# First MLP's second product in seven block products for three of four hidden chunks, and half rows of modulation weights in slots of their own

## The chip, the cores and the metric

One core of a Trainium2 chip runs the whole forward pass of two layers. The metric is the time of one execution on the device in microseconds (us), the median of several runs. The engines named here are TensorE (PE, with its weight loads shown as PEld), VectorE (DVE), ScalarE (ACT), GpSimd (POOL) and SyncE (SP). SP and POOL each have a queue from which transfers are issued.

## The reference, cut to what matters

512 tokens of width 1024 pass through two layers. Layer 0 mixes Fourier channels with neighbourhood attention, layer 1 mixes by pooling, and each layer ends with the same kind of MLP. All numbers are fp32.

```python
def sq_relu_mlp(u, w1, w2):          # u: 512 x 1024, w1: 1024 x 4096, w2: 4096 x 1024
    a = jnp.maximum(u @ w1, 0.0)
    return (a * a) @ w2

for l in range(DEPTH):               # DEPTH = 2
    mod = sc @ w_mod[l] + b_mod[l]   # w_mod[l]: 1024 x 6144
    sh1, sc1, g1, sh2, sc2, g2 = split(mod, 6)
    ...
    h = h + g1 * y                   # y: the mixer's output
    h = h + g2 * sq_relu_mlp(modulate(rms_norm(h, norm2_g[l]), sh2, sc2), w_mlp1[l], w_mlp2[l])
```

A modulation vector `mod` of 1024 numbers is called (l, v) below, v from 0 to 5; (0, 5) is the gate g2 of layer 0.

## The kernel before, in words

Every large product is made of fp32r numbers in two parts: a value is split into a rounded high part (a copy on ACT) and the rest (a subtraction on DVE), and a product is three matmuls, high by high, high by low and low by high (`mm3`, L99 to 103; in the seven-product code the three stand at L1670 to L1672). A matmul has 128 x 128 stationary and 128 x 512 moving numbers where nothing else is said.

The order on each engine is written out by hand. `later` puts a small job on a list with a due time, `tick` (L82) runs at most one due job and then `W.beat()`; both count in `pe[0]`, the matmul time issued so far. `flush` runs all jobs that are left. So jobs and weight splits fall between the matmuls in the order in which the program emits them, and each engine keeps that order.

`Feed` (the object `W`, L113) brings in weights. There are five raw slots of 512 KB (`wr`). `load` issues transfers on SP in the order of `W.items` as long as a slot is free. `one("w")` splits the oldest piece into `wh` (ACT, L204) and `wl` (DVE, L207), and there is room for eight split pieces in the MLPs. `one("m")` takes a row of `w_mod` (128 x 1024, 512 KB): `mac` (L272) multiplies it by the conditioning value and adds it to `macc` on DVE (L278, L280). After eight rows `finish` sums over the partitions with matmuls against ones (L291) and `columns` turns the result with two transposes (L312). `beat` takes a piece when it was issued more than `lead` ago, and a row when the last one is more than `gap` ago. All pieces and rows use the same five raw slots.

The MLP of layer 0 (`mlp`, L1400) goes through four chunks of 1024 hidden units. For each chunk the first product makes eight tiles of 128 hidden units x 512 tokens from 192 matmuls; `act` (L1391) squares them and splits them into `ah` and `al` (DVE L1396, L1397). The second product makes eight tiles of 128 output columns, 192 matmuls again, and `add_h` (L918) adds each one, times the gate, to the token stream `hT`, which is kept transposed (channels on partitions). The last chunk's second product is done in two halves of 256 tokens, so that the next mixer's norm can start.

The MLP of layer 1 (`mlp_blocks`, L1616) writes the second product of each chunk in another way. Its left side, 512 tokens x 1024 hidden units, and its right side are each cut in two by two blocks, and the product is made of seven products of blocks (the Winograd form of Strassen's scheme) in the order "11", "T3", "T1", "T2", "22", "T4", "21", 24 matmuls each. Sums of left blocks are made on DVE in `E` (L1639) and split (`parts`, L96 and L97). Sums of right blocks, that is of weights, are made while they are brought in: a second transfer issued from POOL adds to a raw slot (`add`, L144). The pieces T1, T2 and T4 stand in the same slot one after another: T2's transfer adds to T1's data once that is split, T4's to T2's. The seven results are summed in five accumulators `ac` (L1688 to L1692), with tokens on partitions; at the end the output is stored straight from there, with the token stream turned by `turn` (transposes L1705).

The rows of `w_mod` for the vectors (1, v) are items between the MLP's weights of layer 0.

Of the kernel before, what the change touches and what calls it, by code (L numbers as in the profile page):

```python
# [17 lines left out]
P = 128  # L18
# [20 lines left out]
def body(ctx: ExitStack, tc: tile.TileContext, x, c, cx, c_ctx, w_mod, b_mod, norm1_g, norm2_g,  # L39
# [38 lines left out]

    def later(fn, after=0.0):
# [33 lines left out]
    class Feed:  # L113
# [3 lines left out]
        def __init__(self, nr):  # L117
# [8 lines left out]

            self.place, self.chain = {}, {}
# [19 lines left out]
        def m(self, l, v):  # L147
            for k in range(KT):
                src = w_mod[l, P * k:P * (k + 1), D * v:D * (v + 1)].unsqueeze(1)
                yield ["m", (l, v, k), src, (P, 1, D), None, 0.0]  # L150

        def load(self, n=None):
            while self.loaded < len(self.items) and (n is None or n > 0):
# [29 lines left out]
                if n is not None:  # L183
                    n -= 1

        def one(self, kind, auto=True, eng=None):
# [48 lines left out]
        def beat(self):  # L235

            self.lows()
            for kind in ("w", "m"):
                if not (self.hold and kind == "w") and self.wait[kind] and pe[0] - self.wait[kind][0][5] > self.lead:
# [4 lines left out]
                    elif pe[0] - self.last > (min(self.gap, 2.0) if self.wait["m"][0][1][0:2] == (0, 5) and self.gap < 100 else self.gap):  # L244
# [27 lines left out]
        def mac(self, key, w):  # L272
            l, v, k = key
# [7 lines left out]
            if k == KT - 1:  # L281
                self.fin = (l, v)
                later(lambda: self.fin == (l, v) and self.finish(), {(0, 5): 9.0}.get((l, v), 6.0 if l else 3.5))

        def finish(self):
# [9 lines left out]
            later(lambda: self.columns(l, v, ms), 7.0 if l or v == 5 else 1.5)  # L295
# [13 lines left out]
        def columns(self, l, v, ms):  # L309
            pt = bank("t", "pmvt")  # L310
            for b in range(2):
# [4 lines left out]
                                    bcol(l, v).rearrange("p (g b) -> p g b", g=4), op=ALU.add)  # L316
            if v == 4:
# [876 lines left out]
    W.behind, W.lead = True, 8.0  # L1194
# [7 lines left out]
    Y = Slots(tail, "mz", {"v": 4, "y": 6, "z": 4, "bd": 1})  # L1202
# [105 lines left out]

    def w1_items(l):
        w1v = w1[l].rearrange("(k p) n -> p k n", p=P)  # L1310
        w2v = w2[l].rearrange("(c k p) n -> c p k n", p=P, k=KT)
        for c4 in range(4):
            for q in range(4):
                for e in range(2):
                    c0 = half_columns(c4, q) if l else c4 * 1024 + q * 256
                    yield ("w1", l, c4, q, e), w1v[:, 4 * e:4 * e + 4, c0:c0 + 256], 4, 256, None
            if l:
# [6 lines left out]
    def half_columns(c4, q):  # L1324

        return 2048 * (q % 2) + 512 * c4 + 256 * (q // 2)
# [33 lines left out]
    bd = Y("bd", "bd", shape=(P, 4 * BAND_W))  # L1360
    nc.sync.dma_start(bd, kband)
# [29 lines left out]
    def act(ps, slot):  # L1391
        a, a2 = M("x", "a"), M("x", "a2")
        th, tl = slot("ah"), slot("al")
        nc.scalar.activation(a, ps, AF.Relu)  # L1394
        nc.scalar.activation(th, a, AF.Square)
        nc.vector.tensor_tensor(a2, a, a, op=ALU.mult)  # L1396
        nc.vector.tensor_tensor(tl, a2, th.bitcast(F32), op=ALU.subtract)  # L1397
        return th, tl

    def mlp(l, v, slot, nB, tile_done, half_done, between=None):  # L1400

        vh, vl = v
        waiting = []

        def w1_mm(ps, c4, q, m, c0, c1, ks=range(KT)):
            for k in ks:
                hi, lo = W.get(("w1", l, c4, q, k // 4))
                mm3(ps[:, c0:c1], hi[:, k % 4, m * P:(m + 1) * P], lo[:, k % 4, m * P:(m + 1) * P],
                    vh[k][:, c0:c1], vl[k][:, c0:c1], k == 0, k == KT - 1)
                if k % 2 and k < 6 and c1 == N:  # L1410
                    tick()

        def w2_mm(ps, c4, q, m, ah, c0, c1):
            for k in range(KT):
                hi, lo = W.get(("w2", l, c4, q, k // 4))
                mm3(ps[:, 0:c1 - c0], hi[:, k % 4, m * P:(m + 1) * P], lo[:, k % 4, m * P:(m + 1) * P],
                    ah[k][0][:, c0:c1], ah[k][1][:, c0:c1], k == 0, k == KT - 1)
                if k % 2 and k < 6:
                    tick()

        def free(name, c4, q):
            for e in range(2):
                W.done((name, l, c4, q, e))

        for c4 in range(4):
            ah = []
            first = 0
# [484 lines left out]
```

## Time and profile before

| | |
|---|---|
| median of 3 runs | 1024.47 us (1024.01 to 1027.89) |
| the profiled execution | 1022.89 us, span 1021.0 us |
| PE busy | 993.0 us (97%) |
| DVE busy | 663.2 us (65%) |
| ACT busy | 453.4 us (44%) |
| POOL busy | 121.1 us (12%) |
| moved by DMA | 164.94 MB, 162 GB/s over the span |
| granted TensorE clock | 0.994 |

The layer-0 MLP runs from 287 us to 650 us of the span, the layer-1 MLP from 676 us to the end. Busy times of matmuls overlap, since they are pipelined; the distance from one matmul's start to the next is the better measure. The share of DMA is the mean over 16 DMA engines.

### The profile page before, as it was taken

The page shows a single profiled execution, that of the slowest core. Times are in us where ns is not written, and L with a number is a line of the kernel's source. Part 1 is how long each engine was busy: PE and PEld are TensorE (multiplying, and loading weights), DVE is VectorE, ACT ScalarE, POOL GpSimd, SP SyncE. Part 2 cuts the span into 40 slices and gives each one's busy share as a digit, 9 for nine tenths or more (in the row PEclk, how much of TensorE's full clock was granted, in tenths as well). Part 3 has the DMA queues.
Part 4 walks back from the last instruction along what each step waited for, and adds up shares of the span by engine and source line. Part 5 has one row for each costly group of instructions (what it writes and reads, how often), then busy time and mean ns, then how long its engine had stood idle before and what let it go on. Part 6 is the DMA issues. An engine that isn't in the chain of part 4 may idle for free.

```text
span 1021.0 us, 14020 instructions
## 1 busy us (share of the span) xinstructions
PE 993.0 (97%) x5303; PEld 823.9 (81%) x5303; DVE 663.2 (65%) x993; ACT 453.4 (44%) x787; POOL 121.1 (12%) x153
## 2 busy tenths in 40 slices
PE   6999999899899999999999999999999999999997
PEld 4788788766798888888888889999788888888885
DVE  5667767976578666866755442686563485476868
ACT  5264334676464214322421332667764454453441
POOL 1024103631010000000000000102101101101010
PEclk9999999999999999999999999999999999999999
DMA  9947745213407667676765330126687468478552
GB/s 297 332 145 229 247 145 180 65 24 105 127 22 227 200 215 236 226 242 201 230 221 166 97 110 1 42 84 163 131 231 197 103 182 210 108 162 238 122 113 83
DMA packets 106722, 164.94 MB, mean 162 GB/s; under 512 B 6837, under 2 KB 67909, under 8 KB 106655
## 3 DMA queue, kind: packets, MB, share of 16 engines
q1 hardware_dynamic: 97583, 146.67, 44.3%
q0 software_dynamic: 9072, 17.39, 10.0%
q8 instruction: 41, 0.67, 0.3%
q14 instruction: 26, 0.21, 0.1%
HBM read 161.32 MB, written 2.70 MB: 161 GB/s over the span
## 4 chain that ended last, share of the span: by engine, by line
PE 81%; DVE 7%; DMA 5%; ACT 4%; issue 3%; SPq 0%; POOL 0%; DVEq 0%; ACTq 0%; POOLq 0%
PE pw L100 16%; PE pw L101 16%; PE pw L102 16%; PE pw L1670 4%; PE pw L1671 4%; PE pw L1672 4%; DMA wr<-in_w_mlp 3%; PE pv L1079 2%; DVE wl L207 1%; ACT wh L204 1%; PE pt L1059 1%; PE pwo L100 1%; PE pf L100 1%; PE pj L100 1%; PE pq L100 1%
## 5 line engine op out<-in xcount | busy, mean ns | idle before, releaser
L204 ACT CAST wh<-wr 128x1024 fp32r<-128x1024 f32 x182 | 187.5, 1046 | 162.1 <-DMA wr<-in_w_mlp 97.2
L207 DVE TENSOR_TENSOR wl<-wr,wh 128x1024 fp32r<-128x1024 f32 x178 | 214.7, 1223 | 40.2 <-ACT wh L204 37.4
L100 PE MATMUL pw<-vh,wh 128*128 128x512 f32 (+1 forms) x576 | 212.4, 369 | 0.0
L101 PE MATMUL pw<-vl,wh 128*128 128x512 f32 (+1 forms) x576 | 211.0, 366 | 1.1 <-ACT vl L1291 1.1
L102 PE MATMUL pw<-vh,wl 128*128 128x512 f32 (+1 forms) x576 | 210.6, 366 | 0.0
L101 PEld LDWEIGHTS pw<-vl,wh 128*128 128x128 f32 x576 | 108.6, 189 | 19.1 <-ACT vl L1291 1.7
L100 PEld LDWEIGHTS pw<-vh,wh 128*128 128x128 f32 x576 | 108.6, 189 | 18.2 <-issue 1.2
L102 PEld LDWEIGHTS pw<-vh,wl 128*128 128x128 f32 x576 | 108.6, 188 | 17.7
L100 PE MATMUL pw<-ah,wh 128*128 128x512 f32 (+1 forms) x320 | 112.3, 351 | 0.0
L102 PE MATMUL pw<-ah,wl 128*128 128x512 f32 (+1 forms) x320 | 111.0, 347 | 0.0
L101 PE MATMUL pw<-al,wh 128*128 128x512 f32 (+1 forms) x320 | 111.0, 347 | 0.0
L280 DVE SCALAR_TENSOR_TENSOR macc<-wr,sil,macc 128x1024 f32<-128x1024 f32 x70 | 91.0, 1300 | 0.1
L1672 PE MATMUL pw<-wh,sl 128*128 128x512 f32 x224 | 87.1, 389 | 0.0
L1671 PE MATMUL pw<-wl,sh 128*128 128x512 f32 x224 | 87.1, 389 | 0.0
L1670 PE MATMUL pw<-wh,sh 128*128 128x512 f32 x224 | 87.1, 389 | 0.0
L97 DVE TENSOR_TENSOR sl<-E,sh 128x512 fp32r<-128x512 f32 x56 | 37.6, 689 | 68.2 <-ACT sh L96 68.2
L144 POOL DMA_DIRECT2D wr<-in_w_mlp x32 | 39.1, 1310 | 254.5 <-DMA wr<-in_w_mlp 106.7
L100 PEld LDWEIGHTS pw<-ah,wh 128*128 128x128 f32 x320 | 60.6, 189 | 8.7 <-issue 1.5
L1394 ACT ACTIVATE a<-pw 128x512 f32<-128x512 f32 x32 | 19.1, 598 | 107.7 <-PE pw L102 107.7
L102 PEld LDWEIGHTS pw<-ah,wl 128*128 128x128 f32 x320 | 60.6, 189 | 7.7
L101 PEld LDWEIGHTS pw<-al,wh 128*128 128x128 f32 x320 | 60.6, 189 | 7.5 <-issue 0.2
L918 DVE SCALAR_TENSOR_TENSOR h<-pw,mv,h 128x512 f32<-128x512 f32 (+1 forms) x40 | 25.7, 644 | 57.0 <-PE pw L102 57.0
(265 smaller groups left out, 1600.4 us busy)
## 6 DMA issues: line engine op xcount, KB each, us to landing
wr<-in_w_mlp SPq DMA_DIRECT2D x136, 512.0 KB, 4.6
wr<-in_w_mod SPq DMA_DIRECT2D x80, 512.0 KB, 4.4
wr<-in_w_mlp POOLq DMA_DIRECT2D x32, 512.0 KB, 7.5
wr<-in_w_in_even SPq DMA_DIRECT2D x20, 512.0 KB, 5.9
wm<-in_w_mod SPq DMA_DIRECT2D x32, 256.0 KB, 7.2
wr<-in_w_out_even SPq DMA_DIRECT2D x8, 512.0 KB, 5.2
xn<-in_x SPq DMA_DIRECT2D x8, 256.0 KB, 3.9
out<-acc SPq DMA_DIRECT2D x8, 256.0 KB, 2.4
```

What stands on the lines that cost most here:

```text
L97: (eng or nc.vector).tensor_tensor(lo, src, hi.bitcast(F32), op=ALU.subtract)
L100: nc.tensor.matmul(ps, lh, rh, start=start, stop=False)
L101: nc.tensor.matmul(ps, lh, rl, start=False, stop=False)
L102: nc.tensor.matmul(ps, ll, rh, start=False, stop=stop)
L144: nc.gpsimd.dma_start(it[4], src, accum_op=ALU.add)
L204: nc.scalar.copy(hi, raw)
L207: (eng or nc.vector).tensor_tensor(lo, raw, hi.bitcast(F32), op=ALU.subtract)
L280: nc.vector.scalar_tensor_tensor(self.acc, w[:, 0, :], sil[:, k:k + 1], self.acc, op0=ALU.mult, op1=ALU.add)
L918: nc.vector.scalar_tensor_tensor(hT[d][:, c0:c1], ps[:, p0:p0 + c1 - c0], gate[:, d:d + 1], hT[d][:, c0:c1], op0=ALU.mult, op1=ALU.add)
L1670: nc.tensor.matmul(ps, lh, rh, start=not go, stop=False, skip_group_check=cont)
L1671: nc.tensor.matmul(ps, lh, rl, start=False, stop=False, skip_group_check=cont)
L1672: nc.tensor.matmul(ps, ll, rh, start=False, stop=j == 3, skip_group_check=cont)
```

## The change

- `mlp` and `mlp_blocks` become one function. In layer 0 the chunks 0, 1 and 2 (`BLOCKS = (3, 4)`) now use the seven products for the second product; chunk 3 stays as it was. The pieces of w2 for these chunks come in with the same added transfers as in layer 1.
- During chunk 3 of layer 0, three sums (`together`) and eight jobs (`back`) bring the accumulators home: four transposes of 128 x 128 each, then `add_h` with the gate, or with its negative `minus`.
- The sums of left blocks stand in five places instead of seven (S3 over A21, S1 over A11, S4 over S2); S4 is now made after T2's split (in `parts`), in both layers.
- The rows for (1, 1), (1, 0), (1, 2), (1, 4), (1, 3) are brought in as half rows (256 KB, 80 of them) in four slots of their own (`W.apart`), on SP, once all rows of (0, 5) are issued. Each half of a vector has its own sum, matmuls against ones and transpose. The rows of (1, 5) stay full rows and move into the items of layer 1's MLP.
- `lead` is 7.0 instead of 8.0 in layer 0 (and 7.0 for half rows); `gap` is 1.2, and 4.5 during the seven products, instead of 3.8. Jobs are held back during T2's product (`calm`).
- The table `bd` of the pooling mixer is loaded before chunk 3's second product instead of before the first MLP.

```diff
     def tick():
         for i, (t, fn) in enumerate(jobs):
-            if t <= pe[0]:
+            if t <= pe[0] and not calm[0]:
...
+        def half_rows(self, l, v):
+            for hf in range(2):
+                for k in range(KT):
+                    c0 = D * v + 512 * hf
+                    src = w_mod[l, P * k:P * (k + 1), c0:c0 + 512].unsqueeze(1)
+                    self.rows.append(["m", (l, v, k, hf), src, (P, 1, 512), None, 0.0])
+
+        def load_rows(self):
+            if any(it[1][0:2] == (0, 5) for it in self.items[self.loaded:]):
+                return
+            while self.rows and self.rows_out < self.rows_raws[1]:
+                it = self.rows.pop(0)
+                it[4] = self.rows_raws[0]("wr", "wr", shape=it[3])
+                nc.sync.dma_start(it[4], it[2])
...
-                if not (self.hold and kind == "w") and self.wait[kind] and pe[0] - self.wait[kind][0][5] > self.lead:
+                if not (self.hold and kind == "w") and self.wait[kind] and pe[0] - self.wait[kind][0][5] > (7.0 if self.wait[kind][0][-1] == "apart" else self.lead):
...
+        def finish_half(self, l, v, hf, acc):
+            ps = bank("t", "pmv")
+            for g in range(4):
+                nc.tensor.matmul(ps[32 * g:32 * g + 32, 0:P], ones[:, 0:32], acc[:, P * g:P * g + P],
+                                 start=True, stop=True, tile_position=(0, 32 * g))
...
-    W.behind, W.lead = True, 8.0
+    W.behind, W.lead = True, 7.0
...
-    M = Slots(ctx, "my", {"v": 12, "a": 6, "x": 3})
+    M = Slots(ctx, "my", {"v": 12, "a": 2, "x": 3})
     W.pool(ctx, "wy", 3)
+    W.apart(ctx, 4)
...
+    BLOCKS = (3, 4)
...
-            if l:
+            if c4 < BLOCKS[l]:
                 yield from block_items(l, c4)
                 continue
...
     mods = m0 + m1
+    for v in (1, 0, 2, 4, 3):
+        W.half_rows(1, v)
+    mods = mods[:-6 * KT] + mods[-KT:]
     for l in range(2):
         for i, (key, src, a, b, role) in enumerate(w1_items(l)):
             W.w(key, src, a, b, role)
-            if l or i >= 2:
-                some(mods, 2 if l == 0 and i in (2, 3, 5, 8) else 1)
+            if l == 0 and 2 <= i and len(mods) > KT or l and 8 <= i < 24 and i % 2:
+                some(mods, 1)
...
+        def parts(name, jj):
+            hi, lo = slot("sh", "sl")
+            split(two(left[name], jj), hi, lo)
+            sp.setdefault(name, {})[jj] = (hi, lo)
+            if name == "T2":
+                tt(S2, S2, A12, ALU.subtract, jj)
...
+        def together(a):
+            for i in range(2):
+                nc.vector.tensor_tensor(ac[a][:, i, :], ac[1][:, i, :], ac[a][:, i, :], op=ALU.add)
+
+        def back(d):
+            ps = bank("t", "pbk")
+            for t in range(4):
+                a = ((0, 2), (4, 3))[d // 4][t // 2]
+                nc.tensor.transpose(ps[:, t * P:(t + 1) * P], ac[a][:, t % 2, (d % 4) * P:(d % 4 + 1) * P], ident)
+            add_h(d, ps, mv[l, 5] if d < 4 else minus, 0, N)
...
         for c4 in range(4):
+            blocks = c4 < BLOCKS[l]
...
+                if q == 0 and not blocks:
+                    W.need(l, 5)
+                    minus = small("minus", 8)
+                    nc.vector.tensor_scalar(minus, mv[l, 5], -1.0, None, op0=ALU.mult)
+                    for a in (2, 4, 3):
+                        later(lambda a=a: together(a))
+                    for d in range(KT):
+                        later(lambda d=d: back(d), 14.0)
...
+            W.gap = 4.5
...
+            calm[0] = True
...
             product("T2", B, False, last=sum_b)
+            calm[0] = False
...
             product("21", A, True, last=sum_a)
+            W.gap = 1.2
```

More of the change, by code (lines that the diff above doesn't have):

```diff
@@ L243, in beat @@
                         pass
-                    elif pe[0] - self.last > (min(self.gap, 2.0) if self.wait["m"][0][1][0:2] == (0, 5) and self.gap < 100 else self.gap):
+                    elif pe[0] - self.last > self.gap:
                         self.one("m")
@@ L1389, in body, with mlp @@
                 W.one("w")
[L1391 to L1400, printed above, removed]
+    bd = None
+    def mlp(l, v, nB, slot, between=None):
+        nonlocal Y, bd
         vh, vl = v
-        waiting = []
+        A11, A21, A12, A22, S2 = range(5)
+        left = {"11": A11, "T3": A21, "21": A12, "T1": A11, "T2": S2, "T4": A22, "22": S2}
         def w1_mm(ps, c4, q, m, c0, c1, ks=range(KT)):
@@ L1423, in free, with into, store, stream @@
                 W.done((name, l, c4, q, e))
+        def into(acc, i, ps, op=ALU.add, fresh=False):
+            if fresh:
+                nc.scalar.copy(acc[:, i, :], ps)
+            elif op == ALU.subtract:
+                nc.vector.tensor_tensor(acc[:, i, :], acc[:, i, :], ps, op=op)
+            else:
+                nc.vector.tensor_tensor(acc[:, i, :], ps, acc[:, i, :], op=op)
+        def store(acc, i, t, b):
+            nc.sync.dma_start(out[0, t * P:(t + 1) * P, 512 * b:512 * b + 512], acc[:, i, :])
+        def stream(t, b):
+            return HT[:, 4 * b:4 * b + 4, t * P:(t + 1) * P]
+        def turn(k):
+            ps = bank("t", "pht")
+            for t in range(4):
+                nc.tensor.transpose(ps[:, t * P:(t + 1) * P], hT[k][:, t * P:(t + 1) * P], ident)
+            nc.scalar.copy(hT[k], ps)
+        def base(a, i, t, b, op):
+            acc, g = ac[a][:, i, :], mv[l, 5][:, 512 * b:512 * b + 512]
+            nc.vector.tensor_tensor(acc, acc, g, op=ALU.mult)
+            wide = acc.rearrange("p (k n) -> p k n", k=4)
+            nc.vector.tensor_tensor(wide, stream(t, b), wide, op=op)
         for c4 in range(4):
+            sp = {}
+            blocks = c4 < BLOCKS[l]
+            final = blocks and c4 == 3
             ah = []
-            first = 0
             if c4 == 0:
@@ L1469, in mlp @@
-            if c4 == 3 and half_done:
+                        W.gap, W.hold = 1.2, False
+            done = 2 if c4 == 0 else 0
+            for q in range(4):
+                if q >= done:
+                    for m in range(2):
+                        ps = bank("m", "pw1")
+                        w1_mm(ps, c4, q, m, 0, N)
+                        if blocks:
+                            act(ps, q, m)
+                        else:
+                            ah.append(act_split(ps))
+                        if m:
+                            free("w1", c4, q)
+                        tick()
+                    if blocks:
+                        sums(q)
+                if q == 0 and not blocks:
[6 more added lines that the diff above has]
+                        later(lambda d=d: back(d), 14.0)
+                if final and q == 0:
+                    W.need(l, 5)
+                    for a, t, b, op in ((0, 0, 0, ALU.add), (3, 2, 1, ALU.subtract), (2, 2, 0, ALU.add), (4, 0, 1, ALU.subtract)):
+                        for i in range(2):
+                            later(lambda a=a, i=i, t=t, b=b, op=op: base(a, i, t + i, b, op))
```

459 lines of the change are left out of this document (212 added, 247 removed).

## The prediction

> **What bounds the kernel now.** I read first the page's busy times and slices, then the chain of work that ended last, then the busy times of stages that I set at the seams between first and second products, and last the order of matmuls, splits and transfers inside one stage.
>
> ```profile
> PE 993.0 (97%) x5303; PEld 823.9 (81%) x5303; DVE 663.2 (65%) x993; ACT 453.4 (44%) x787; POOL 121.1 (12%) x153
> PE   6999999899899999999999999999999999999997
> DVE  5667767976578666866755442686563485476868
> DMA  9947745213407667676765330126687468478552
> PE 81%; DVE 7%; DMA 5%; ACT 4%; issue 3%; SPq 0%; POOL 0%; DVEq 0%; ACTq 0%; POOLq 0%
> ```
>
> No slice of PE is below 9 from the 12th to the 39th, and 81% of the chain is PE. The stages say the same. Columns: stage, its length, busy time of PE, PEld, DVE, ACT, POOL, granted clock, DMA share, GB/s.
>
> ```profile
> 320.00:565.00 245.00, 245.00 (x1110) 198.38 (x1109) 160.33 (x178) 71.80 (x87) 0.00 (x0) 1.00 0.66 215
> 423.70:468.20 44.50, 44.50 (x203) 36.24 (x202) 30.28 (x33) 12.70 (x13) 0.00 (x0) 1.00 0.74 245
> 559.20:602.70 43.50, 43.50 (x193) 36.03 (x192) 20.91 (x25) 15.31 (x21) 0.00 (x0) 1.00 0.31 97
> 730.50:768.60 38.10, 38.10 (x170) 31.56 (x169) 26.38 (x30) 24.68 (x34) 2.44 (x2) 1.00 0.73 192
> 812.10:850.20 38.10, 38.10 (x170) 31.56 (x169) 31.44 (x39) 21.09 (x26) 2.45 (x2) 1.00 0.75 194
> 850.20:893.70 43.50, 43.50 (x194) 36.03 (x193) 16.43 (x19) 18.04 (x26) 7.30 (x6) 1.00 0.60 144
> 893.70:931.80 38.10, 38.10 (x170) 31.53 (x169) 31.24 (x39) 21.00 (x26) 2.45 (x2) 1.00 0.73 188
> ```
>
> In layer 0's MLP (first three rows) PE is busy all the time at clock 1.00. The last four rows are layer 1's: a second product as seven products takes 38.1 us there, in the same matmul stream without gaps, while DVE is busy 31 of the 38 us. So PE sets the time of layer 0's MLP, and matmuls taken out there are time saved, as long as what feeds PE keeps up. That layer 1 already runs the new form at full pace is the best evidence for it; what layer 0 has on top are the rows of `w_mod`.
>
> **The matmuls removed.** The pace is the distance between starts, not the 389 ns of one.
>
> ```profile
> L1670 PE MATMUL pw<-wh,sh x56: 389/389/389, 893.7 to 931.1; 128*128 128x512 f32 x56
> L100 PE MATMUL pw<-ah,wh x64: 389/389/499, 423.6 to 467.6; 128*128 128x512 f32 x64
> L291 PE MATMUL pmv<-macc,kc x8: 379/391/403, 438.7 to 439.0; 128*32 128x256 f32 x8
> ```
>
> Line 1670 is every third matmul: 55 steps in 37.4 us are 0.680 us for three, 0.2267 each. Three chunks go from 192 to 168 matmuls: 72 x 0.2267 = 16.3 us less. [...]
>
> **Matmuls added.** `back` is eight times four transposes, the kind that `turn` (L1705) does in layer 1:
>
> ```profile
> 707.97 0.39 PE L102 MATMUL pw<-vh,wl 128*128 128x512 f32 x1
> 708.21 0.60 PE L1705 MATMUL pht<-kc,h 128*128 128x128 f32 x4
> 708.56 0.48 PE L100 MATMUL pw<-vh,wh 128*128 128x512 f32 x1
> 708.87 0.40 PE L101 MATMUL pw<-vl,wh 128*128 128x512 f32 x1
> ```
>
> From 708.21 to 708.56 are 0.35 us, and the next step is 0.31 instead of 0.23, so about 0.45 with both edges: 8 x 0.48 = 3.9 us with a little for waiting on a bank. The five vectors (1, v) are summed in ten halves instead of five wholes. The 64 matmuls `ah` by `wh` above hold one whole sum (the L291 row, and its two transposes): 44.0 us against 63 x 0.680 = 42.8, so 1.1 us each. A half has as many matmuls against ones, half as wide, and one transpose instead of two. If width decides, ten halves cost what five wholes did (0 more); if each insertion costs the same, 5.5 us more. Eight records within 0.6 us stand nearer to a cost per matmul than per column, so I take 3.4. Sum on PE: -16.3 + 3.9 + 3.4 = -9.0 us (-12.4 to -6.9).
>
> **DVE and ACT.** Per changed chunk DVE loses 16 instructions of `act` and 8 `add_h`, and gains 14 low parts, 8 sums, 14 additions to accumulators and 6 more weight splits:
>
> ```profile
> L1397 DVE TENSOR_TENSOR al<-a,ah x32: 692/693/694, 304.6 to 604.3; 128x512 fp32r<-128x512 f32 x32
> L918 DVE SCALAR_TENSOR_TENSOR h<-pw,mv,h x7: 746/751/752, 429.4 to 463.0; 128x512 f32<-128x512 f32 x7
> L97 DVE TENSOR_TENSOR sl<-E,sh x56: 680/692/694, 701.0 to 1007.9; 128x512 fp32r<-128x512 f32 x56
> L207 DVE TENSOR_TENSOR wl<-wr,wh 128x1024 fp32r<-128x1024 f32 x178 | 214.7, 1223 | 40.2 <-ACT wh L204 37.4
> L280 DVE SCALAR_TENSOR_TENSOR macc<-wr,sil,macc x33: 1276/1279/1285, 379.9 to 547.4; 128x1024 f32<-128x1024 f32 x33
> ```
>
> That is 16 x 0.69 + 8 x 0.75 = 17.1 us less and 36 x 0.69 + 6 x 1.22 = 32.2 more, 15 us per chunk (some 7 less in chunk 0, where ACT copies ten of the fourteen). A half row's step is not in the trace; between 0.64 (half of 1.28) and 0.75 I take 0.72. Weights and sums alone keep DVE at (31.44 + 16.43) / 81.6 = 59% by the layer-1 rows; the 80 half rows, some 56 us over about 245, bring 81%. Inside a seven-product stage, with a half row every 5.4 us (the gap of 4.5 in steps of the beat): 31.4 + 7 x 0.72 = 36.5 of 38.1 us. PE covers that, barely. ACT at 21 to 25 of 38 is no bound. In chunk 3, `together` and `back` add 6 x 0.69 + 8 x 0.75 = 10 us to DVE's 20.9 of 43.5, with the last half rows beside: covered. S4 made later takes a sum out of the way of T2's split and puts it where DVE waits: nothing.
>
> **Transfers.** A chunk reads 13 MB instead of 8. Layer 1's rows show the price: 0.75 and 0.60 of the engines, 0.67 over the pair of stages, at fewer GB/s than layer 0 moves at 0.74, because the adding transfers from POOL are dear. The half rows are 21 MB; at 215 GB/s for a share of 0.66 they need 64 us of all engines, 0.26 of 245 us. Together 0.93, against 0.66 before. They have slots of their own, so they no longer hold the five raw slots; but the same engines carry them. [...]
>
> **Where PE would wait first.** Weights are split eight pieces ahead. The left parts are not. In product "22" of layer 1's third chunk:
>
> ```profile
> 912.12 1.05 ACT L204 CAST wh<-wr 128x1024 fp32r<-128x1024 f32 x1 [3.32 <-DMA wr<-in_w_mlp]
> 913.08 1.13 ACT L96 CAST sh<-E 128x512 fp32r<-128x512 f32 x2
> 913.20 1.23 DVE L207 TENSOR_TENSOR wl<-wr,wh 128x1024 fp32r<-128x1024 f32 x1 [2.54 <-ACT wh L204]
> 914.95 1.29 DVE L97 TENSOR_TENSOR sl<-E,sh 128x512 fp32r<-128x512 f32 x2
> 915.44 0.39 PE L1670 MATMUL pw<-wh,sh 128*128 128x512 f32 x1
> 915.89 0.40 PE L1672 MATMUL pw<-wh,sl 128*128 128x512 f32 x1
> DMA to landing us min/median/max: 5.7/7.5/12.5
> ```
>
> ACT waits 3.32 us for T4's second adding transfer, and behind it stand the splits for "22". The first `sl` is done at 914.95 + 0.69 = 915.64; its matmul starts at 915.89. The margin is 0.25 us. In layer 0 two half rows (256 KB, 0.8 us of all engines each) fall into the ten microseconds of T4's transfers, which is 1.6 us later for ACT; a half row's 0.72 us on DVE is hidden in DVE's own 2.54 us of waiting. Less the margin that is 1.35 us of waiting on PE where both half rows go ahead of the adding transfers, and none where they don't; I take the middle, 0.7 us for each of three chunks. The last row is POOL's transfers from issue to landing; 5 us more than the median on both links, T2 and T4, is the upper bound, 10 us per chunk; none is the lower, as PE's stream has no gap to win back.
>
> **The rest.** The rows of (1, 5) move eight transfers of 512 KB and 8 x 1.28 = 10 us of DVE into layer 1's first chunks, into the shared slots; DVE at 26.38 of 38.10 covers it, the DMA share there goes from 0.73 to about 0.95: 0.4 us. Its matmuls only move. The table `bd`:
>
> ```profile
> 262.21 2.98 DMA bd<-kband
> 264.14 1.03 ACT L204 CAST wh<-wr 128x1024 fp32r<-128x1024 f32 x1
> 265.20 1.23 DVE wl L207
> ```
>
> It stands in the chain for 3 us, but the split at 265.20 needs `wh`, done at 265.17, so its going gains nothing. On SP its new place waits for the last `back`, with loads behind it, while DMA is at 0.31 and below: nothing. Half rows at one per 2 us (four slots, 7 us and a beat each) in first products and one per 5.4 us in second ones are through by about 570 us; they are needed at about 655.
>
> **Sum.** -9.0 + 3 x 0.7 + 0.4 = -6.5 us against the profiled execution's 1022.9: 1016.4. The median of the runs, 1024.5, is 1.6 above that execution, so 1018.0 for the median.
>
> **Rivals.** *Nothing waits.* Layer 1 lives with a margin of 0.25 us and has no gap, and half rows may fall behind the adding transfers; against it stands the share of 0.93. [...] Then -9.0: 1015.5, down to 1012 if half sums cost no more than whole ones. *DVE full.* DVE runs without idle time from 913.2 in the stage above; with four half rows (2.9 us) in its second half that can't be hidden, and the bank jobs, each chunk's second product is some 2.7 us late: -9.0 + 8.1 gives about 1023.5, no change. For it speaks 36.5 of 38.1; against it that wl splits run ahead and can slip. *The adding chain ends last, slower.* T2 and T4 go over three transfers in a row on engines at 0.93; if each link takes 12.5 instead of 7.5 us, "22" is late by almost 10 us per chunk: 29 - 9 = +20, 1044. It outweighs the gain from 3 us per chunk, 2 us per link. Against it: half rows are few in these stages, and loads that wait for slots give way.
>
> **How the numbers follow.** Forecast 0.50 (1015.5 to 1020.5 as the waits are 0 to 5 us), nothing waits 0.20, DVE full 0.19, the adding chain 0.11. Half a per cent, 5.1 us, is about what a measurement can tell here: faster is below 1019.3, which takes four fifths of the forecast and all of the second case, 0.60; slower 0.11; same 0.29. The range, 1012 to 1027, leaves out most of the last case and the ends.
>
> **What would show it.** Right: layer 0's second products of chunks 0 to 2 last 38 to 40 us instead of 44.5, with gaps only at "22" behind an ACT wait on a transfer; chunk 3's first product about 4 us longer; DVE at 0.8 and DMA at 0.9 from 320 to 560 us. Wrong: gaps of PE before "T2", "T4" or first products, DVE-ended waits of whole microseconds, half rows still collected when the mixer begins, or a longer end of layer 1.

## The result and the profile after

After: 1031.22 us, median of 9 runs (1028.55 to 1033.12); before, on the same chip, 1024.35 (1021.20 to 1027.89). The ratio is 1.0065, 95% interval [1.0048, 1.0082]: the change costs 0.65%. The forecast was 1018.0 with a range of 1012 to 1027, and faster at 0.60; both miss. The profiled execution after has a span of 1031.3 us, 10.3 more than before; it is the longest of the nine (1033.12), and that of before (1022.89) lies 1.5 under the median here, so the traces below differ by 3.4 us more than the medians.

The page of after, the lines that answer to those shown of before:

```profile
PE 991.1 (96%) x5303; PEld 816.5 (79%) x5303; DVE 712.4 (69%) x1102; ACT 498.3 (48%) x857; POOL 149.9 (15%) x177
PE   6999999899899799999999999999999999999997
DVE  5567768976676595797689853686584394476778
DMA  9947745112318999789888430127887578477562
PE 59%; DVE 16%; DMA 12%; issue 6%; ACT 6%; SPq 1%; POOL 0%; DVEq 0%; POOLq 0%; ACTq 0%
```

PE's slices still look full; one digit has fallen to 7. The chain tells more: PE's share fell from 81% to 59%, and DVE and DMA hold 28% of it where they held 12%. The stages, at the seams of after (columns: length, busy PE, PEld, DVE, ACT, POOL, granted clock, DMA share, GB/s); the second to the fourth are the new second products, the fifth is chunk 3's first product, the last is layer 1's chunk 0:

```profile
320.00:565.00 245.00, 235.21 (x1067) 187.78 (x1066) 186.92 (x252) 114.98 (x154) 29.14 (x24) 0.99 0.90 255
335.30:381.80 46.50, 41.10 (x172) 32.57 (x171) 35.87 (x44) 29.01 (x40) 6.01 (x5) 0.96 0.95 237
427.20:468.70 41.50, 39.33 (x180) 31.85 (x179) 36.82 (x52) 21.09 (x26) 2.42 (x2) 1.00 0.84 232
513.60:557.70 44.10, 41.88 (x187) 32.69 (x186) 39.20 (x55) 21.09 (x26) 2.71 (x3) 0.96 0.86 237
557.70:607.20 49.50, 48.99 (x243) 39.34 (x242) 37.75 (x56) 15.34 (x21) 0.00 (x0) 1.00 0.50 166
736.70:780.70 44.00, 41.74 (x174) 33.35 (x173) 28.76 (x35) 24.57 (x34) 3.65 (x3) 0.96 0.76 210
```

A seven-product stage has 38.1 us of matmuls; these take 46.5, 41.5 and 44.1, with PE idle for 2 to 5 us in each, and layer 1's chunk 0, which the change was to leave at 38.1, takes 44.0. DVE (0.76) and DMA (0.90) are at the shares that were forecast, but with waits of PE.

The table gives each stage as the distance, in the timeline, from its first matmul to the next stage's first; "1st" and "2nd" are first and second products, c the chunk, and 2nd c3 includes the mixer behind it. The columns with experiments are explained below.

| stage | before | after | e1 | e8 | e9 | e11 |
|---|---|---|---|---|---|---|
| 2nd c0 | 44.87 | 46.45 | 41.98 | 43.22 | 40.50 | 40.37 |
| 1st c1 | 44.59 | 45.47 | 43.52 | 45.46 | 43.52 | 44.59 |
| 2nd c1 | 44.59 | 41.48 | 38.08 | 39.07 | 38.08 | 38.11 |
| 1st c2 | 45.26 | 44.85 | 43.52 | 44.85 | 43.52 | 44.59 |
| 2nd c2 | 45.70 | 44.16 | 38.08 | 39.54 | 38.08 | 39.73 |
| 1st c3 | 43.52 | 49.51 | 47.27 | 49.54 | 47.27 | 51.01 |
| 2nd c3 | 72.88 | 72.92 | 72.90 | 72.91 | 72.85 | 76.03 |
| layer 1, 1st c0 | 54.89 | 56.52 | 55.14 | 55.97 | 55.67 | 56.05 |
| layer 1, 2nd c0 | 38.08 | 43.99 | 48.09 | 42.13 | 38.08 | 38.08 |
| layer 1, 1st c2 | 43.52 | 43.52 | 43.52 | 43.52 | 45.24 | 45.24 |

From before to after, the second products of layer 0 gained 3.1 us where 20.9 were there to gain (135.2 before, 114.2 without waits and sums of rows), its first products lost 6.5, layer 1's beginning lost 7.5. The MLP begins 1.1 later (it begins at 286.2 to 288.4 us in all the kernels here), and the end behind the last matmul is 1.7 shorter, a gain that was not forecast. Its cause is open: this end takes 7.8 us before and 6.1 after, but 7.2 and 7.5 in e2 and e6, whose code is the same there.

Line numbers are those of the changed kernel: L332 adds a half row, L314 a whole one, L1524 sums left blocks, L99 is the split's low part, L1585 to L1587 the three matmuls of a block product, L353 a half sum's transpose, L1605 and L1607 add to the accumulators, L233 casts a weight piece.

How a wait comes about is seen in chunk 2, in DVE's timeline (start, length, engine, line, operation, then in brackets the idle time before it and what ended it) and in the waits of PE in the same stage:

```profile
513.35 1.62 DVE L332 SCALAR_TENSOR_TENSOR macc<-wr,sil,macc 128x512 f32<-128x512 f32 x2
518.24 0.75 DVE L332 SCALAR_TENSOR_TENSOR macc<-wr,sil,macc 128x512 f32<-128x512 f32 x1 [3.27 <-DMA wr<-in_w_mod]
518.91 1.41 DVE L1524 TENSOR_TENSOR E<-E 128x512 f32<-128x512 f32 x2
...
536.01 0.75 DVE L332 SCALAR_TENSOR_TENSOR macc<-wr,sil,macc 128x512 f32<-128x512 f32 x1
536.68 0.68 DVE L1607 TENSOR_TENSOR acc<-pw,acc 128x512 f32<-128x512 f32 x1
537.28 1.28 DVE L99 TENSOR_TENSOR sl<-E,sh 128x512 fp32r<-128x512 f32 x2
```

```profile
PE pmvt L353 <- DVE acc L1605: 1.1, 1, 1.1
PE pw L1587 <- DVE sl L99: 1.1, 1, 1.1
```

A half row has not landed when its add reaches the head of DVE's queue at 514.97. DVE stands for 3.27 us, and the sums behind it, whose input ACT has finished at 515.02, stand too, with the splits behind them. DVE then works without a pause, but for 0.69 us, until PE waits (it is busy 39.2 of the stage's 44.1 us): twenty microseconds later "22" wants a split that is late. That the two belong together was tried in e7 and e8. Layer 1's chunk 0 has a longer chain with a row of (1, 5). DVE's timeline there, then POOL's adding transfers in this stage, before and after, and PE's wait:

```profile
740.81 1.28 DVE L314 SCALAR_TENSOR_TENSOR macc<-wr,sil,macc 128x1024 f32<-128x1024 f32 x1 [3.94 <-DMA wr<-in_w_mod]
```

```profile
737.16 2.44 POOL L144 DMA_DIRECT2D wr<-in_w_mlp  x2 [8.68 <-DVE wl L207]
746.59 2.44 POOL L149 DMA_DIRECT2D wr<-in_w_mlp  x2 [8.10 <-DVE wl L236]
```

```profile
PE pw L1587 <- DVE sl L99: 2.3, 1, 2.3
```

The 3.94 us are not the whole chain here, as DVE catches up. But POOL's last adding transfers are issued 9.9 us into the stage, where before it was 6.7, and the cast that reads them is 3.0 us later in the stage too; DVE stands 2.39 us for it, and then an add of 1.28 us runs ahead of the split that "22" wants. How much of POOL's delay comes from the add's wait, and how much from the rows in the raw slots ahead of it, is not shown; without the row all of it is gone (e3).

In chunk 1 a half row's add waits 2.73 us in the same way, and behind it the copy of a half sum (L348) that holds the bank of T2; PE's wait in that stage:

```profile
PE pw L1585 <- DVE ms L348: 2.2, 1, 2.2
```

Chunk 0 begins with another chain, on ACT: PE's waits in the stage, and ACT's for weights from 300 us on.

```profile
PE pw L1585 <- ACT a L1516: 3.9, 1, 3.9
PE pw L1586 <- DVE wl L236: 1.4, 1, 1.4
```

```profile
ACT wh L233 <- DMA wr<-in_w_mlp: 24.0, 11, 9.0
```

A cast stands 9.0 us at the head of ACT's queue for its piece, up to 337.98, and the activations of the last tiles behind it: their matmuls have ended by 335.48, and the next activation starts at 341.45.

### The profile page after: what moved, and what is told of

The parts are those of the page before. It is cut to its first block, busy times and chain, and to the rows that moved or that the text cites. A ratio compares the mean times of both kernels' runs of the same rounds, so it can differ in the third digit from the quotient of the medians.

```text
span 1031.3 us, 14337 instructions
## 1 busy us (share of the span) xinstructions
PE 991.1 (96%) x5303; PEld 816.5 (79%) x5303; DVE 712.4 (69%) x1102; ACT 498.3 (48%) x857; POOL 149.9 (15%) x177
## 3 DMA queue, kind: packets, MB, share of 16 engines
q1 hardware_dynamic: 98831, 149.82, 44.2%
## 4 chain that ended last, share of the span: by engine, by line
PE 59%; DVE 16%; DMA 12%; issue 6%; ACT 6%; SPq 1%; POOL 0%; DVEq 0%; POOLq 0%; ACTq 0%
PE pw L102 8%; PE pw L103 8%; PE pw L104 8%; DMA wr<-in_w_mlp 7%; DVE wl L236 5%; PE pw L1587 4%; PE pw L1585 4%; DMA wr<-in_w_mod 4%; PE pw L1586 4%; ACT wh L233 2%; DVE macc L332 2%; PE pv L1158 2%; DVE sl L99 1%; DVE macc L314 1%; DVE acc L1607 1%
## 5 line engine op out<-in xcount | busy, mean ns | idle before, releaser
L236 DVE TENSOR_TENSOR wl<-wr,wh 128x1024 fp32r<-128x1024 f32 x196 | 236.2, 1220 | 46.5 <-ACT wh L233 46.3
L233 ACT CAST wh<-wr 128x1024 fp32r<-128x1024 f32 x200 | 206.1, 1047 | 127.4 <-DMA wr<-in_w_mlp 75.9
L1585 PE MATMUL pw<-wh,sh 128*128 128x512 f32 x392 | 155.9, 398 | 6.1 <-ACT a L1516 3.9
L1587 PE MATMUL pw<-wh,sl 128*128 128x512 f32 x392 | 155.0, 395 | 3.5 <-DVE sl L99 3.3
L1586 PE MATMUL pw<-wl,sh 128*128 128x512 f32 x392 | 154.7, 395 | 1.4 <-DVE wl L236 1.4
L99 DVE TENSOR_TENSOR sl<-E,sh 128x512 fp32r<-128x512 f32 x98 | 65.6, 686 | 79.1 <-ACT sh L98 79.0
L1585 PEld LDWEIGHTS pw<-wh,sh 128*128 128x128 f32 x392 | 74.9, 191 | 23.3 <-ACT a L1516 4.3
L1587 PEld LDWEIGHTS pw<-wh,sl 128*128 128x128 f32 x392 | 74.7, 191 | 20.9 <-DVE sl L99 5.1
L1586 PEld LDWEIGHTS pw<-wl,sh 128*128 128x128 f32 x392 | 74.6, 190 | 17.4 <-DVE wl L236 1.8
L98 ACT CAST sh<-E 128x512 fp32r<-128x512 f32 x98 | 58.5, 618 | 54.8 <-DVE E L1524 54.1
L332 DVE SCALAR_TENSOR_TENSOR macc<-wr,sil,macc 128x512 f32<-128x512 f32 x70 | 52.3, 747 | 20.0 <-DMA wr<-in_w_mod 19.3
L1524 DVE TENSOR_TENSOR E<-E 128x512 f32<-128x512 f32 x56 | 38.6, 689 | 24.5 <-ACT E L1518 23.6
L314 DVE SCALAR_TENSOR_TENSOR macc<-wr,sil,macc 128x1024 f32<-128x1024 f32 x35 | 46.4, 1326 | 7.3 <-DMA wr<-in_w_mod 7.1
```

The source lines that it names most:

```text
L98: nc.scalar.copy(hi, src)
L99: (eng or nc.vector).tensor_tensor(lo, src, hi.bitcast(F32), op=ALU.subtract)
L233: nc.scalar.copy(hi, raw)
L236: (eng or nc.vector).tensor_tensor(lo, raw, hi.bitcast(F32), op=ALU.subtract)
L332: nc.vector.scalar_tensor_tensor(acc, w[:, 0, :], sil[:, k:k + 1], acc, op0=ALU.mult, op1=ALU.add)
L1585: nc.tensor.matmul(ps, lh, rh, start=not go, stop=False, skip_group_check=cont)
```

## The experiments

Two theories. A: the rows beside the seven products do it; an add that is queued before its transfer has landed blocks DVE, and PE waits behind it. B: the seven products can't be fed in layer 0, rows or not. C, a variant: the transfers crowd each other, and DVE's order plays no part. Line numbers shift by a few between kernels.

**e1, no half rows.**

```diff
-    for v in (1, 0, 2, 4, 3):
-        W.half_rows(1, v)
+    for v in (1, 0, 2, 4, 3):
+        r = small(f"mv1{v}", 8)
+        nc.vector.tensor_copy(r, bcol(1, v))
+        W.scaled(1, v, r)
```

> The half rows of layer 1's modulation (80 transfers, 80 adds on DVE, ten sums) are left out; these five rows hold the bias alone. The gate row of layer 0 and the last row of layer 1 stay. After is 1031.2 us. Theory A (rows beside the seven products hold DVE up, and PE waits and drops to half clock behind it): the ten sums' own PE work goes (10 x 0.67 = 6.7 us), the wait of chunk 1 (2.2) and the waits and the half-clock window of chunk 2 (5.0) go, chunk 0 stays at 46.4 us: 1017 us (1015 to 1020), with the seven products of chunks 1 and 2 at 38.1 to 39.5 us. Theory B (the seven products of layer 0 can't be fed, rows or not): only the 6.7 us go, chunks 1 and 2 stay at 41 to 44 us: 1024.5 us.

1016.60 us, 0.9925 of before [0.9906, 0.9944], as theory A expected. Chunks 1 and 2 run at 38.08 us without any wait: B falls for them. Chunk 0 keeps 42.0 (46.4 was expected). Layer 1's chunk 0 is worse, 48.1 instead of 44.0 us: the full rows there are untouched, and why they cost more is not shown (in the other runs with rows in this place the stage takes 41.8 to 45.9 us).

**e7 and e8, one half of the load each.** In e7 the half rows are transferred and not added, in e8 added and not transferred.

```diff
 # e7
             if k == 0:
-                nc.vector.tensor_scalar(acc, w[:, 0, :], sil[:, k:k + 1], None, op0=ALU.mult)
-            else:
-                nc.vector.scalar_tensor_tensor(acc, w[:, 0, :], sil[:, k:k + 1], acc, op0=ALU.mult, op1=ALU.add)
+                nc.vector.memset(acc, 0.0)
 # e8
-                it[4] = self.rows_raws[0]("wr", "wr", shape=it[3])
-                nc.sync.dma_start(it[4], it[2])
+            wide = ident.unsqueeze(1).to_broadcast([P, 4, P])     # stands for w in both operations
```

> All 80 half rows are transferred as in after, at the same points, but DVE neither reads nor adds them (the accumulator is set to zero once a half row's turn begins; the ten sums on PE stay), so those five rows hold the bias alone. Theory A (DVE's order): as no add waits for a landing any more, chunks 1 and 2 fall to 38.7 to 39.5 us, 1023 us (1021 to 1026). Theory C (crowded transfers): weights still come late beside the half rows, chunks 1 and 2 stay at 41 to 44 us, 1029 to 1031 us.

> The 80 adds on DVE and the ten sums stay where they are in after, but read a constant that is always in SBUF; the half rows are not transferred. Theory A (DVE's order): no add waits, chunks 1 and 2 at 38.7 to 39.5 us, 1023 us (1021 to 1026), as in the run with transfers alone. Theory C (crowded transfers): 1023 us too, but then the run with transfers alone is at 1029 to 1031. If DVE's sheer load is the bound (58 us of adds more), this one stays at 1029 to 1031 us and the run with transfers alone is at 1023.

e7: 1024.78 us (1.0006 of before [0.9993, 1.0019]); e8: 1021.26 (0.9974 [0.9960, 0.9988]). e7's chunks 1 and 2 take 40.72 and 39.54 us, with a single wait of 1.4 us between them; e8's take 39.07 and 39.54, with none. The rest above 38.08 is the half sums' own matmuls. Both totals are those of theory A. After has 4.4 us of waits in these two chunks: adds alone leave none, transfers alone the 1.4 us, in chunk 1 behind a half sum's copy. Most of the waits need both together, which is what theory A says and C does not. (Where nothing is added, no add keeps a slot from the next load either; e7 does not part the two.) DVE is not too full either. e8's stages of chunks 1 and 2:

```profile
421.80:460.90 39.10, 39.10 (x181) 31.81 (x179) 37.33 (x53) 21.36 (x26) 2.42 (x2) 1.00 0.71 182
505.80:545.40 39.60, 39.60 (x188) 31.86 (x187) 38.14 (x54) 21.30 (x26) 2.42 (x2) 1.00 0.74 189
```

DVE is busy 37.33 of 39.10 and 38.14 of 39.60 us, and PE has no gap. The adds' own groups show the difference: idle time of DVE just before them, after first and then e8:

```profile
L332 DVE SCALAR_TENSOR_TENSOR macc<-wr,sil,macc 128x512 f32<-128x512 f32 x70 | 52.3, 747 | 20.0 <-DMA wr<-in_w_mod 19.3
```

```profile
L331 DVE SCALAR_TENSOR_TENSOR macc<-kc,sil,macc 128x512 f32<-128x512 f32 x70 | 52.4, 749 | 0.9
```

In chunk 0 it is otherwise: 46.89 us with transfers alone, 43.22 with adds alone. There the half rows' transfers themselves cost some 4 us: SP issues the first four at 320 to 322 us, right ahead of seven weight pieces. Whether they hold the weights up in SP's queue or on the DMA engines is open.

**e4, half rows without the seven products.** Layer 0 keeps plain second products; the rows stay as in after.

```diff
-    BLOCKS = (3, 4)
+    BLOCKS = (0, 4)
```

> Layer 0 keeps the plain second products in all four chunks, as before; the half rows, the gate row of layer 0 in the raw slots and the last row in layer 1 stay as in after. Before is 1024.4 us. Theory A in its strong form (the rows cost whatever stands beside them): the sums' 3.4 us, layer 1's 5 us and some 3 us of waits in layer 0's chunks 0 to 2: 1033 to 1036 us. Theory A in its weak form (only the seven products are tight enough): the 3.4 and the 5 us: 1033 us at most, 1031 at least, layer 0's plain second products at 44.6 to 45.5 us. Theory B (rows harmless): 1027 to 1028 us.

1034.23 us, 1.0099 of before [1.0084, 1.0114]. The number is that of theory A's strong form, the stages are not: from 1st c1 to 1st c3 they add up to 224.2 us against 223.7 before. The loss stands where the gate row and the row of (1, 5) are: 4.1 us in chunk 0, whose plain product needs the gate at once where the seven products need it in chunk 3, and 7.5 at layer 1's beginning. Beside plain products the half rows land in time:

```profile
L332 DVE SCALAR_TENSOR_TENSOR macc<-wr,sil,macc 128x512 f32<-128x512 f32 x70 | 52.2, 746 | 2.2 <-DMA wr<-in_w_mod 1.8
```

2.2 us of waiting where after has 20.0. The median half row takes 3.6 us from issue to landing here and 5.6 in after: beside the seven products' transfers they land later, and only then do their adds hold DVE up.

**e3, the row of (1, 5) later.**

```diff
-            if l == 0 and 2 <= i and len(mods) > KT or l and 8 <= i < 24 and i % 2:
+            if l == 0 and 2 <= i and len(mods) > KT or l and 44 <= i < 52:
```

> The eight full rows of layer 1's last modulation vector are moved from the second product of chunk 0 to the first product of chunk 2 of layer 1. Theory A: layer 1's chunk 0 second product falls from 44.0 to 38.1 us; 1.7 us of that is the row's own sum, which moves with it, the rest (2.3 of wait, 1.8 of half clock) is gained: 1027 us (1026 to 1028.5). Theory B has no part in layer 1, whose chunks were 38.1 us before: it expects the 4 us too, unless the rows only carry their waits along to chunk 2, which would leave 1031 us.

1027.48 us (1.0038 of before [1.0025, 1.0050]): 3.7 us less than after. Layer 1's chunk 0 is back at 38.08 us, and the first product of its chunk 2 takes 45.24 instead of 43.52, the row's own sum and no wait. DVE even stands 12.0 us there for the bias of this row, and PE for nothing. Where nothing behind the row on DVE is due soon, the same eight transfers and adds cost only their matmuls.

**e2, the gate row of layer 0 as half rows; e5, a longer lead; e6, both and more.** Three attempts to keep the half rows and mend their place.

```diff
 # e2: the row of (0, 5) first among the half rows, none in the raw slots
+    W.half_rows(0, 5)
+    mods = [it for it in mods[:-6 * KT] if it[1][0:2] != (0, 5)] + mods[-KT:]
 # e5, in beat
-  (7.0 if self.wait[kind][0][-1] == "apart" else self.lead)
+  ((12.0 if self.gap > 4.0 else 7.0) if self.wait[kind][0][-1] == "apart" else self.lead)
 # e6: e2 and e3, gap 3.5, and in beat (quiet: last quarter of a first product, T1 to 22)
+  ((12.0 if self.quiet else 7.5) if self.wait[kind][0][-1] == "apart" else self.lead)
```

> The gate row of layer 0, whose eight full rows took turns with the weight pieces in the five raw slots at chunk 0, becomes the first 16 half rows in the slots of their own; the raw slots then hold weights alone. Theory A: chunk 0's pieces of sums start earlier, its second product falls from 46.4 to 39 to 41 us, and its half-clock window goes; chunks 1 and 2 keep their waits, and a few half rows move from chunk 2 to chunk 3: 1025 us (1023 to 1028). Theory B (cold start: the first adding transfers of a layer are late whatever is loaded beside them): chunk 0 stays above 44 us: 1030 us or more.

> Within the seven products a half row is added on DVE no earlier than 12 of the kernel's own microseconds after its transfer was issued (7 in after, and still 7 in the first products). All transfers, adds and sums stay. After is 1031.2 us. Theory A, in its exact form (an add that is placed before its half row has landed blocks DVE's queue, and the splits of sums behind it come late): chunk 1's wait of 2.2 us and chunk 2's 5.0 us (waits and half clock) go, 1024 us (1023 to 1027), chunks 1 and 2 at 39 to 40 us. Theory C (the transfers crowd each other, whatever the order on DVE): the waits stay, 1029 to 1032 us.

> Everything is computed, with the rows placed anew: layer 0's gate row as the first 16 half rows (the raw slots then hold weights alone from chunk 0 on); a half row is added 12 of the kernel's microseconds after its issue in the last quarter of a first product and from T1 to 22, 7.5 elsewhere; layer 1's last row in the first product of its chunk 2. Theory A: chunk 0 at 39 to 41 us (46.4 in after), chunks 1 and 2 at 39 us (41.5 and 44.2), layer 1's chunk 0 at 38.1 us (44.0, 1.7 of it moved): 1031.2 - 6.5 - 2.5 - 5.2 - 4.2 = 1013 us (1010 to 1018). Theory B or C: no less than 1025 us.

1035.73 us (1.0106 [1.0080, 1.0132]), 1029.59 (1.0066 [1.0043, 1.0088]) and 1026.91 (1.0027 [1.0014, 1.0040]). What theory A expected fails in all three, and the times are those that its rivals B and C gave; what speaks for A here is in the traces alone. e6's gain over after is e3's part of it. Chunk 0 got worse, 49.7 us in e2 and 52.2 in e6. DVE's timeline in e2 at the seam into chunk 0's second product, and PE's waits there:

```profile
329.68 0.75 DVE L330 SCALAR_TENSOR_TENSOR macc<-wr,sil,macc 128x512 f32<-128x512 f32 x1 [5.45 <-DMA wr<-in_w_mod]
...
336.81 0.75 DVE L330 SCALAR_TENSOR_TENSOR macc<-wr,sil,macc 128x512 f32<-128x512 f32 x1 [2.46 <-DMA wr<-in_w_mod]
337.48 0.68 DVE L99 TENSOR_TENSOR sl<-E,sh 128x512 fp32r<-128x512 f32 x1
```

```profile
PE pw L1586 <- DVE sl L99: 2.7, 1, 2.7
```

The gate row had gone from the raw slots, but half rows now stood in front of the splits of "11". In e5 the add that hurts was queued in the last first-product tile, where the lead was still 7: DVE waits 2.72 us for it before 432.24, and chunk 1 takes 43.6 us. Chunk 2 falls from 44.2 to 40.3 us with 0.4 us of waiting left, near A's 39 to 40 us and not what C gave. e6 had 12 in that tile as well, and DVE still stood 5.13 us for a half row at the start of chunk 0's second product. With four slots a late add makes the next load late (SP stands for half rows' adds 36.4 us in after and 40.8 us in e5, from 380 to 560 us), so a lead counted when the program is written does not hold. Moving a wait on DVE was not enough; fewer transfers had to stand there.

**e9, no rows in layer 0's MLP.** The gate (0, 5) and the five vectors of the half rows hold the bias alone; (1, 5) as in e3.

```diff
...
-        W.half_rows(1, v)
-    mods = mods[:-6 * KT] + mods[-KT:]
+    mods = mods[-KT:]
```

> Layer 0's gate row is left out too, with its transfers, adds and sum, as are the half rows: six modulation rows hold the bias alone, and weights are all that layer 0's MLP loads. Layer 1's last row stands in chunk 2. What is asked is chunk 0 of layer 0, whose second product stayed at 42.0 us with the half rows gone. Theory A (its rest is the gate row's full rows in the raw slots): chunk 0 falls to 38.1 to 39 us; with layer 1's chunk 0 at 38.1 the whole is at 1004 us (1002 to 1006). Theory B (the first chunk can't be fed from a cold start: its adding transfers begin together and crowd each other): chunk 0 stays at 41 to 43 us, 1008 us.

1003.52 us, 0.9811 of before [0.9796, 0.9826]. The stages of chunks 0 and 1:

```profile
333.90:374.40 40.50, 39.27 (x169) 31.23 (x169) 30.84 (x36) 26.85 (x38) 4.85 (x4) 1.00 0.78 200
417.90:456.00 38.10, 38.10 (x170) 31.56 (x169) 32.39 (x40) 21.41 (x26) 2.42 (x2) 1.00 0.78 201
```

So of chunk 0's 8.4 us over 38.1, 6.0 belong to rows and 2.4 to a cold start (the stage itself differs by 1 to 2 us from run to run: 46.45 in after, 48.02 in e3, whose layer 0 is the same). The total is A's; chunk 0's 40.5 us lie between the two forecasts, and B is left with 2.4 us.

**e10 and e11, whole rows again, in other places.** All vectors are computed; no half rows, none in chunk 0.

```diff
 # e11: rows between the weight pieces, counted per piece of the first products of c1, c2, c3; c3's w2 at the end
+            if l == 0 and i >= 22:
+                some(mods, {1: (2, 2) + (1,) * 6, 2: (2, 2) + (1,) * 6,
+                            3: (1,) * 4 + (0,) * 4 + (0, 3, 3, 3, 3, 4, 4, 4)}[i // 22][i % 22] if i % 22 < (16 if i >= 66 else 8) else 0)
+            elif l and 44 <= i < 52:
+                some(mods, 1)
```

> Everything is computed. The half rows are undone: layer 0's gate row and five of layer 1's rows are whole rows in the five raw slots again, placed between the weight pieces of the first products of chunks 1, 2 and 3 (12, 12 and 8 transfers) and of chunk 3's plain second product (16); none stands in chunk 0. Layer 1's last row stands in chunk 2. Theory A (rows do no harm where nothing behind them on DVE is due): chunks 1 and 2 at 38.1 to 40 us, chunk 0 as in the run without rows, six sums of 1.1 us where half sums of 0.67 stood: 1010 us (1006 to 1016). Theory C (any row beside weights with adding transfers makes them late): the waits come back in chunks 1 and 2 at 41 us or more, 1018 us or more.

> Everything is computed; whole rows in the raw slots as in the run with full rows (span 1018.0 us), but ten instead of twelve between the weight pieces of the first products of chunks 1 and 2, doubled at the first pieces rather than the last, four in that of chunk 3, and 24 in chunk 3's plain second product; a row's sum is put on PE 6 of the kernel's microseconds after its last add instead of 3.5. Theory A: the waits that were left in chunks 1 and 2 (4.0 and 2.4 us over 38.1) came from weight pieces queued behind rows and from whole-row adds (1.3 us each) in front of splits; they halve, and chunk 3's first product (52.7 us) loses the 1.5 us wait at its row sum and the 1.9 us before its turns back: 1015 us (1012 to 1018). If the place of the rows doesn't matter, only their number: 1020 us, no change.

e10: 1019.97 us (0.9969 [0.9957, 0.9981]), some 10 above what A expected and in C's range (1018 or more): chunks 1 and 2 took 42.1 and 40.5 us, where C gave 41 or more. ACT stands 20.3 us for weight pieces from 412 to 462 us; that these stood behind rows in the raw slots is the reading on which e11 was built. e11: 1017.17 us (0.9931 [0.9915, 0.9946]), as expected within 2, faster than before and 14 us faster than after, with all of the change's seven products and everything computed. Its second products in chunks 0 to 2:

```profile
332.80:373.10 40.30, 38.97 (x169) 31.18 (x168) 30.23 (x35) 24.32 (x35) 4.85 (x4) 1.00 0.77 197
417.70:455.80 38.10, 38.10 (x169) 31.48 (x168) 32.88 (x42) 17.59 (x23) 4.88 (x4) 1.00 0.77 194
500.40:540.10 39.70, 38.70 (x169) 31.38 (x168) 34.50 (x43) 19.75 (x26) 4.87 (x4) 1.00 0.75 190
```

DVE waits 0.8 us in all for its 70 full-row adds in the whole kernel:

```profile
L314 DVE SCALAR_TENSOR_TENSOR macc<-wr,sil,macc 128x1024 f32<-128x1024 f32 x70 | 91.3, 1304 | 0.8 <-DMA wr<-in_w_mod 0.3
```

The price is 3.1 us in chunk 3's second product, where 24 rows stand.

**e12, e11 with a short lead for weights.**

```diff
+                        W.lead = 4.0
                         if l:
                             while stage:
                                 stage.pop().close()
                             tail.close()
-                            W.lead = 4.0
```

> As the run before it in this call, and in layer 0, from the last half of chunk 0's first piece on, a weight piece is cast 4 of the kernel's microseconds after its issue, as layer 1 does, where after waits 7. The seven products of layer 1's chunk 0 took 38.1 us with that lead and no rows; those of layer 0's chunk 0 took 40.5 us with no rows and the lead of 7. Theory: the cold start's 2.4 us in chunk 0 are that lead: chunk 0 falls from 41 to 38.5 us, chunks 1 and 2 gain slack, 1011 us (1008 to 1015). If the cold start is the crowd of adding transfers: no change in chunk 0, 1015 us.

1038.10 us, 1.0133 of before [1.0117, 1.0150]: the theory falls, and the other way. ACT's waits for weights in layer 0's MLP and the mixer, e11 first:

```profile
ACT wh L233 <- DMA wr<-in_w_mlp: 91.9, 40, 9.4
```

```profile
ACT wh L233 <- DMA wr<-in_w_mlp: 116.2, 41, 10.5
```

A cast that is queued 3 us earlier does not find its piece 3 us earlier; it stands in ACT's queue, in front of activations and splits, and chunk 0 takes 44.9 us instead of 40.4. The largest part of the loss, 8.8 us, is in chunk 3's second product with the mixer behind it (84.9 us instead of 76.0). That it is theory A's mechanism on another engine is argued from these waits, not tested. What makes the 2.4 us of the cold start is left open.

## Why the prediction was wrong, by its own steps

- **Matmuls removed: right.** 0.2267 us a matmul; without waits a second product is 38.08 instead of 43.52 us (e1, e9).
- **`back`: right.** 47.27 - 43.52 = 3.75 us (e9), forecast 3.9. **Half sums: too dear.** The stages from 1st c1 to 1st c3 are 8.0 us longer in e8 than in e1, 0.7 of it a wait: 0.73 each, against 1.07 for a whole one (1st c1 of e11): 1.9 us more in all, forecast 3.4. PE's sum was to be -9.0 and comes to about -10.7, within its bounds. From there to the 10.3 us more of the trace are 21 us: some 7.0 in chunks 1 and 2, 8.4 in chunk 0 and 5.8 at layer 1's beginning.
- **Transfers, "they have slots of their own, so they no longer hold the five raw slots; but the same engines carry them": the step that failed.** The share (0.93 forecast, 0.90 measured) was right. It was turned into a delay for weights only. What a late half row does to its own reader was not asked: its add stands in DVE's queue, placed 7 of the kernel's microseconds after the issue, while the prediction's own row for POOL's adding transfers said 5.7/7.5/12.5 (the half rows took a median of 5.6 us, and 7.9 from 420 to 432 us, around chunk 1's late add). "A half row's 0.72 us on DVE is hidden in DVE's own 2.54 us of waiting" priced the add (0.75 us in fact) and not its wait (20.0 us over the MLP).
- **Where PE would wait first: wrong place, wrong size.** Forecast: "22", 0.7 us per chunk, behind an ACT wait. Measured: 2.2 us at T2 in chunk 1, twice 1.1 us around "22" in chunk 2, 3.9 us at "11" and 1.4 at T2 in chunk 0. "22" is among them in chunk 2 and in layer 1's chunk 0 (2.3 us), but behind DVE, not ACT.
- **Chunk 0 had no term of its own.** The gate row's pieces in the raw slots, the half rows and the first adding transfers meet there; 8.4 us over 38.1. Here weights do come late, as the prediction thought, but by more: 9.0 us for one cast, where it had 1.6.
- **The rows of (1, 5): 0.4 us forecast, 3.7 us by e3.** "DVE at 26.38 of 38.10 covers it" is the same mistake: a share of busy time covers the length of an add, not its wait for a landing. **`bd`**: nothing that can be seen, as forecast.
- **The rivals.** *Nothing waits*: true of the seven products alone in chunks 1 and 2 (e1, e9). Not of after: there, at 255 GB/s, transfers were late enough to block DVE (20.0 us ahead of its half rows' adds). *DVE full*: falls with e8. *The adding chain ends last* had the right sign for another reason. The sign that was to show the prediction wrong, "DVE-ended waits of whole microseconds", is what came.

## What to carry to other kernels

In these traces DVE and ACT stand behind an instruction whose transfer has not landed, though work behind it is ready (3.27 us on DVE, 9.0 us on ACT). So an instruction that reads a transfer must be costed as its length plus the chance that the transfer lands late, and charged to everything queued behind it. Ask of each transfer that is added or moved which instruction reads it, how long after its issue, against the slowest landings under the load that the change itself makes. If rows must pass, put them where nothing behind them is due soon (e3, e11), rather than give them buffers and a lead (e5, e6).

## What the runs showed of the hardware

Behind three waits of PE in after the granted TensorE clock was 0.50 or 0.51. Stretches of after (columns as above; the clock is the third number from the end):

```profile
342.60:346.00 3.40, 3.40 (x9) 2.66 (x9) 2.04 (x4) 1.15 (x2) 0.20 (x1) 0.51 1.08 307
540.60:544.00 3.40, 3.40 (x10) 2.62 (x9) 3.40 (x7) 0.66 (x2) 0.00 (x0) 0.50 0.82 232
762.40:765.80 3.40, 3.40 (x10) 2.61 (x9) 3.40 (x4) 1.76 (x3) 0.00 (x0) 0.51 0.70 224
447.00:451.00 4.00, 4.00 (x19) 3.29 (x18) 3.17 (x6) 3.51 (x5) 0.00 (x0) 1.00 0.91 297
```

At clock 0.50 a matmul starts every 0.43 us (seven steps from 540.84 to 543.83) where it is 0.2267 at 1.00. What a stretch costs is seen in PE's timeline in chunk 2, the first and the last two rows:

```profile
540.43 0.61 PE L1585 MATMUL pw<-wh,sh 128*128 128x512 f32 x1
540.84 0.63 PE L1586 MATMUL pw<-wl,sh 128*128 128x512 f32 x1
...
550.11 0.39 PE L1587 MATMUL pw<-wh,sl 128*128 128x512 f32 x1
550.43 0.43 PE L345 MATMUL pmv<-macc,kc 128*32 128x128 f32 x8
```

36 matmuls lie between 540.43 and 550.43, 10.00 us where 36 x 0.2267 = 8.2 would do: 1.8 us, and three such stretches are some 5 of the 10.3 us. They follow on PE waits of 3.9, of 1.1 and 1.1 within four microseconds, and of 2.3 us; a wait of 2.2 us in chunk 1 is followed by full clock (last of the four rows above). They differ in where they fall. The clock drops at 342.64, 540.62 and 762.48 us and is full again 3.4 us later each time. With the drops of the same trace at 199.28 and 1028.72 the distances are 143.36, 197.98, 221.86 and 266.24 us, which is 42, 58, 65 and 78 steps of 3.413 us (143.36 / 42) to within 0.03 us, as on a fixed grid. The windows of such a grid ahead of the drops at 540.62 and 762.48, and the two windows that share chunk 1's wait:

```profile
537.21:540.62 3.41, 1.47 (x6) 0.95 (x7) 3.41 (x6) 3.41 (x6) 0.00 (x0) 1.00 0.87 283
759.07:762.48 3.41, 1.17 (x5) 0.99 (x6) 3.41 (x5) 3.41 (x5) 0.00 (x0) 1.00 0.66 195
441.63:445.04 3.41, 2.88 (x19) 1.72 (x17) 3.39 (x6) 1.05 (x1) 0.00 (x0) 1.00 1.08 234
445.04:448.45 3.41, 1.76 (x8) 1.49 (x9) 2.69 (x5) 0.96 (x2) 0.00 (x0) 1.00 1.07 370
```

PE is idle for 1.94 and 2.24 us of the first two windows, for 0.53 and 1.65 us of the others, and for 2.86 us ahead of the drop at 342.64. So in after's seven-product stages the clock fell behind windows with 1.94 us or more of idle PE and stayed full behind those with 1.65 or less. No threshold is shown by that: ahead of the MLP it fell behind 1.68 us as well (195.87 to 199.28).

So a wait of PE cost more than its length here: the 2.2 us of chunk 2's two waits came with 1.8 us of half clock, 4.0 in all.
